# Unused pads in on-chip memory, so that the operands of the float32r products start 128 bytes apart, modulo 256

## The chip, the cores and the metric

The kernel runs on one core of a Trainium2 chip. The time is device time in microseconds (us), from the first to the last instruction of that core and the little that lies around them; lower is better. Everything on the chip that this text speaks of is inside one core: the tensor engine (PE), which multiplies matrices; the vector engine (DVE), ScalarE (ACT) and GpSimd (POOL), which work element by element; the queues that start transfers (SP and others); and the on-chip memory of 128 partitions, in which every tile has a start address that is the same in all partitions.

## The reference

Two layers of a decoder trunk on 512 tokens of 1024 channels, in float32. Cut to what matters here:

```python
for i in range(DEPTH):                                  # 2 layers
    n = rmsnorm(h, mix_norm[i])
    u = n @ w_in[i]                                     # 1024 -> 2304, four token mixers
    a_val, a_gate, pool_in, q, k, v, gb, gc, sv = jnp.split(u, IN_SPLITS, axis=-1)
    ...
    mixed = jnp.concatenate([y_a, y_b, y_c, y_d], axis=-1)
    h = h + mixed @ w_out[i]
    h = h + hier_moe(rmsnorm(h, ffn_norm[i]), ...)      # 16 experts of width 256, two per token
    gate = jax.nn.sigmoid(rmsnorm(h, ple_norm[i]) @ ple_gate_w[i] + ple_gate_b[i])
    h = h + gate * (p[i] @ ple_proj[i])
return rmsnorm(h, final_norm)
```

## The kernel before

Large products are made in float32r: each operand is split in two tiles, hi (the rounded value) and lo (the rest), and one product becomes three matmuls (`mm3`, lines 247 to 250): hi by hi (line 248), hi by lo (249) and lo by hi (250). Each matmul first loads a stationary operand of 128 columns and then streams the moving operand, 512 columns (or 256 in the first projections and for v), past it into a bank of results.

Weights come from DRAM in units of [128, 2048], through rings of buffers `wr` (`wraw`, and up to three more rings while the experts run). ScalarE makes `wh` from a half of a unit (`whi_of`, line 221) and DVE makes `wl` as the difference (`wlo_of`, line 232). There are four `wh` and four `wl` tiles of 4096 bytes per partition, in the pools `whi` and `wlo`, and the stream `_Weights.get` makes them a few halves ahead.

A layer has these stages, and the products in them are:

- `project`: the normed input `nhi`, `nlo` by the weights. The channel-major part (`cm_half`) has the weights stationary and `nhi`/`nlo` moving; v, q and k have it the other way round. Between the products DVE does the convolution's taps (line 474).
- `attend`: attention, and the output projection between its steps, with `mhi`/`mlo` stationary and the weights moving.
- `experts`: for each of 16 experts eight chunks of gate and up weights by the gathered rows `xTh`/`xTl` (24 matmuls, rows stationary), then the down product, of which the first chunk is split (`hh` stationary, 6 matmuls) and the second is plain float32 (line 1231).
- `combine`: the embedding's gate, with `n3h`/`n3l` stationary and the weights moving.

The order on every engine is written out by hand in tables and doesn't depend on addresses. Addresses come from tile pools, which are stacked from either end of the memory. `base`, `gpool`, `small`, `wraw`, `whi` and `wlo` lie on the left and stay open throughout; the pools of the stages lie behind them on the left, or on the right. `self.side` says which, and it is turned round after each layer (line 355: `self.side = self.side[::-1]`), so what lies left in layer 0 lies right in layer 1.

Of the kernel before, what the change touches and what calls it, by code (L numbers as in the profile page):

```python
# [11 lines left out]
F32 = mybir.dt.float32  # L12
# [21 lines left out]
# columns of the packed per-layer parameters  # L34
# [4 lines left out]
# columns of the shape constants  # L39
K_ID, K_RC, K_IO, K_VT, K_DE, K_IW, K_MK, K_TRI, K_COS, K_SIN = 0, 128, 160, 288, 304, 320, 322, 450, 578, 834  # L40
NCON, NCON2, NCON3 = 322, 256, 512
NOIDX = 2048.0
BUDGET = 3.1
# [7 lines left out]
# the order in which work is issued: of an attention step, of the last steps, of the layer's end  # L51
# [18 lines left out]
class _Pool:  # L70
    """A tile pool that is opened at once and closed by name."""
# [12 lines left out]
class _Weights:  # L84
    """The stream of weight units, in the order in which they are used.

    A unit is [128, 2048] in DRAM. A split half is handed out as a pair of float32r tiles (hi, lo)
    whose sum is the weight; what is left of the unit is handed out as it is.
    """
# [10 lines left out]
    def add(self, src, split=2, gain=None):  # L100
        """split: of the halves, how many; gain: called for a column of factors for each quarter of the unit."""
        u = len(self.units)
        self.units.append((src, split))
        self.gains[u] = gain
        self.items += [(u, a) for a in range(split)] + [(u, None)] * (split < 2)
# [41 lines left out]
class _Ticks:  # L147
    """Work for later ticks, and background work that is dealt out by its length."""
# [18 lines left out]
class _Kernel:  # L167
# [7 lines left out]

    def mm(self, shape, dt=F32):
        return self.ps.tile(shape, dt, name="mm", tag="mm", bufs=8 - self.ntr - self.attn)
# [4 lines left out]
    def banks(self, ntr, attn=0):  # L182
        """The PSUM's banks anew: ntr for transposes, one for attention's result, the others for products."""
        if self.ps:
            self.ps.close_()
        self.ntr, self.attn = ntr, attn
        self.ps = self.pool("ps", space=PSUM)

    # ---- small pieces
# [10 lines left out]
    def rms(self, i):  # L200
        """1 / rms of the rows of token tile i."""
        ss = self.sm.tile([128, 1], F32, name="ss", bufs=4)
        self.SC.activation(self.junk, self.h[i], AF.Square, accum_out=ss)
        r = self.sm.tile([128, 1], F32, name="r", bufs=4)
        self.rsq(r, ss, 1.0 / D)
        return r
# [45 lines left out]
    # ---- the whole  # L252
    def run(self):
# [5 lines left out]
        self.rings = []  # L259
        self.whi = self.pool("whi", 4)  # L260
        self.wlo = self.pool("wlo", 4)
        self.ps = None
# [9 lines left out]
        # the functions' table is loaded, and the tensor engine's clock up, by the time the data is there  # L272
# [68 lines left out]
        for p in (self.dram, self.ps, self.wlo, self.whi, ring, self.sm, self.gpool, base):  # L341
            p.close_()
# [18 lines left out]
    def params(self, l):  # L361
        V, SC, P = self.V, self.SC, self.P
        lam_init = 0.8 - 0.6 * math.exp(-0.3 * l)
        sm = self.sm
        self.cwh = sm.tile([128, 2, 31], F32, name="cwh", bufs=1)
        V.tensor_scalar(self.cwh, P[:, C_CW:C_CW + 62].rearrange("p (m k) -> p m k", m=2), 0.5, None, op0=ALU.mult)
        lgh = sm.tile([128, 4], F32, name="lgh", bufs=1)
        V.tensor_scalar(lgh, P[:, C_LG:C_LG + 4], 0.5, None, op0=ALU.mult)
        self.lg, self.lb = lgh[:, 0:2], lgh[:, 2:4]
        self.sgl = sm.tile([128, 1], F32, name="sgl", bufs=1)  # L370
        V.tensor_scalar(self.sgl, P[:, C_SG:C_SG + 1], 1.0 - lam_init, None, op0=ALU.mult)
        lamp = self.xp.tile([128, 2, 32], F32, name="lamp", bufs=1)
        lv = P[:, C_LAM:C_LAM + 128].rearrange("p (c a d) -> p c a d", c=2, a=2)
        V.tensor_mul(lamp, lv[:, :, 0], lv[:, :, 1])
        lam2 = sm.tile([128, 2], F32, name="lam2", bufs=1)
        V.tensor_reduce(lam2, lamp, axis=AX, op=ALU.add)
        SC.activation(lam2, lam2, AF.Exp)
        self.nlam = sm.tile([128, 1], F32, name="nlam", bufs=1)
        V.tensor_sub(self.nlam, lam2[:, 1:2], lam2[:, 0:1])
        V.tensor_scalar(self.nlam, self.nlam, -lam_init, None, op0=ALU.add)  # L380
        self.pbs = sm.tile([128, 2], F32, name="pbs", bufs=1)
        V.tensor_mul(self.pbs, P[:, C_PB:C_PB + 2], P[:, C_PS:C_PS + 2])
        self.cb = P[:, C_CB:C_CB + 2]
        self.psc = P[:, C_PS:C_PS + 2]
        self.sw = P[:, C_SW:C_SW + 6].rearrange("p (m k) -> p m k", m=2)
        self.rb = P[:, C_RB:C_RB + 20]
        self.pw = P[:, C_PW:C_PW + 256].rearrange("p (m c) -> p m c", m=2)
        # the router's weights, times the gain of the norm before it
        self.rw = P[:, C_RW:C_RW + 160].rearrange("p (c e) -> p c e", c=8)
        V.tensor_mul(self.rw, self.rw, P[:, C_FN:C_FN + 8, None].to_broadcast([128, 8, 20]))  # L390

    # ---- input projection; the channel-major mixers
# [9 lines left out]
    def cm_first(self, o, halves, toks):  # L402
        """As cm_half for both halves, the products of the high parts before the others."""
# [18 lines left out]
    def project(self):  # L422
# [3 lines left out]
        # conformer gate and value, the first two token tiles before the others  # L426
# [59 lines left out]
        # pooling mixer  # L486
# [4 lines left out]
        sums = []  # L491
# [47 lines left out]
        # short gated convolution  # L539
# [35 lines left out]
        # v, q and k by token; rotary  # L575
# [41 lines left out]
        def rotate(i, b):  # L617
            """Rotary on a token tile's q or k; the first tile is read where the products stand."""
# [18 lines left out]
    def layer_norm(self):  # L637
        """LayerNorm over the channels of the convolution's result, and silu, tile by tile in stages."""
        V, T, SC, tk, acc, sm = self.V, self.T, self.SC, self.ticks, self.acc, self.sm
        mv, rs, th = {}, {}, {}  # L640
        # token-major values stand in the tile's own columns once these are transposed
# [41 lines left out]
    # ---- differential attention, with the output projection between  # L683
    def attend(self):
# [9 lines left out]
        # a head's 32 channels of q, split, stand as hi, lo, hi, and those of k as hi, hi, lo  # L694
# [85 lines left out]
        def comb(n):  # L780
            """The difference of the two softmaxes, times the first one's sum."""
# [72 lines left out]
        def fn2(i):  # L854
            """The rows of the normed tile, for the experts' gathers."""
            p, tag = ((self.gpool, "gv0"), (xp, "qks"), (tp, "xn"), (xp, "xt"))[i]
            xx = self.scaled(i, rr[i], gffn, p, 1, "xn", tag)
            SC.dma_start(xnd[i * 128:(i + 1) * 128, :], xx)

        def fn3(i, b=None):  # L860
            """The tile itself transposed, for the router, whose result is scaled afterwards."""
# [18 lines left out]
        # the pieces of the output projection, each in two halves, and the step from which each may go  # L880
# [5 lines left out]
        def filler(n, k):  # L886
            """Up to k half pieces."""
# [38 lines left out]
        def turns(n):  # L926
            if n == NS:
                kp.close_()
                self.mp = self.pool("mp", side=self.side[0])
                self.open_ring(NRING2, 0, NRING2)  # L930
# [32 lines left out]
        # the last tile, whose chain of results the rest gives way to  # L963
# [49 lines left out]
    def open_ring(self, n, side, first):  # L1013
        """More room for weights, up to the end of the experts."""
        w, end = self.w, self.moe_end[self.l]
        if not self.rings:
# [3 lines left out]
            def pick(u):  # L1020
                """The room that is free first, of that which is there; the last units leave the first ring."""
# [10 lines left out]
    def warm(self, k):  # L1032
        """Products that only keep the tensor engine's clock up where it would wait."""
# [4 lines left out]
    # ---- routing  # L1038
# [3 lines left out]
    def first_max(self, dst, src, n, nm):  # L1042
        """One-hot of the first largest of each n groups' four elements, and the largest."""
# [10 lines left out]
    def route(self):  # L1054
# [10 lines left out]
        # the first largest of the groups, and the first two of every group's experts  # L1065
# [12 lines left out]
        # pc: of the tokens before, how many go to each expert; last, of all tokens  # L1078
# [5 lines left out]
        # what a slot shall know of its token: the rows in xnd and in yd, less NOIDX  # L1084
# [20 lines left out]
        # blocks past the first 128 rows of an expert  # L1105
# [15 lines left out]
    def weights(self):  # L1121
        """Weights of a token's two experts."""
# [20 lines left out]
    def block(self):  # L1143
        """The next block past the first rows: its tokens' rows in xnd and yd, and its expert."""
# [15 lines left out]
        # block cnt holds the pairs with ob = cnt + 1 that are past their expert's first rows  # L1160
# [35 lines left out]
    def silu(self, gu):  # L1196
        """2 silu(gate) * up."""
# [7 lines left out]
    def down_in(self, hs, split=True):  # L1205
        """The hidden values transposed, the first half of the channels in two parts."""
# [12 lines left out]
    def down(self, hT, w_, first=None):  # L1219
        """Half of the product with the down weights, w_(chunk) each; or the first chunk's two parts."""  # L1220
# [49 lines left out]
    # ---- the experts, on the first 128 rows of each  # L1270
# [47 lines left out]
    # ---- combine, per-layer embedding gate, and the next norm  # L1318
    def combine(self):
# [10 lines left out]
        def proj(k):  # L1330
            """The embedding's projection, halved, in pieces."""
# [42 lines left out]
        def norm2(i):  # L1374
            """1 / rms of the rows again, from the sums of the halves."""
# [191 lines left out]
```

## Time and profile before

| | |
|---|---|
| Time, median of 3 runs (lowest to highest) | 928.54 us (927.61 to 929.37) |
| Span of the profiled execution | 928.2 us |
| PE busy | 860.4 us (93%) |
| DVE busy | 715.7 us (77%) |
| ScalarE busy | 520.2 us (56%) |
| GpSimd busy | 150.0 us (16%) |
| Moved by DMA | 179.02 MB, 193 GB/s over the span |
| TensorE clock granted, mean | 0.971 of full speed |

How to read it: the profile is one execution, taken by the hardware profiler. Matmuls are pipelined, so that the next one starts long before the one before it has ended; the busy time of a group is the sum of durations shared out where they overlap, and "mean ns" is the duration of one. PEld is the load of the stationary operand, which runs beside matmuls. PEclk is the granted clock of TensorE, 1.00 or 0.50 of full speed (2.4 or 1.2 GHz). The span is divided between the two layers at about 467 us: layer 0's projection from 15 to 126 us, attention to 237, experts to 390, the rest to 467, and then the same again.

### The profile page before, as it was taken

What the parts mean: (1) busy time and instruction counts of PE and PEld (TensorE: products, weight loads), DVE (VectorE), ACT (ScalarE), POOL (GpSimd) and SP (SyncE); (2) the same over time, 40 slices, a digit from 0 to 9 for tenths busy, and PEclk for the clock granted to TensorE, in tenths of its full rate; (3) what the DMA queues carried; (4) which work ended last, traced back from release to release, by engine and by line L of the source; (5) the groups of instructions that cost most, each with busy time, mean ns of one, the idle gap of its engine ahead of it and who ended that gap; (6) DMA issues with size and microseconds to landing.
All of it is one profiled execution on the core that took longest, in us unless ns stands there. A gap on an engine that the chain in (4) does not pass through costs nothing. (4 is left out here: it accounts for less than half of the span.)

```text
span 928.2 us, 12348 instructions
## 1 busy us (share of the span) xinstructions
PE 860.4 (93%) x4393; PEld 687.8 (74%) x4393; DVE 715.7 (77%) x1182; ACT 520.2 (56%) x945; POOL 150.0 (16%) x214
## 2 busy tenths in 40 slices
PE   7999988897899999989979999989969999998994
PEld 5888876686677777767879887767847777776783
DVE  4599989966788888746676998998478888885674
ACT  4322246863687878745433232488337778786453
POOL 1040001122322211101010400022131222111201
PEclk8999999998999999999999999999979999999998
DMA  9322330148799979663322223110968998873602
GB/s 351 107 91 91 102 113 1 46 175 324 265 336 373 360 281 336 227 231 146 114 91 91 91 90 108 64 46 25 350 232 304 368 374 318 324 304 99 249 24 90
DMA packets 35775, 179.02 MB, mean 193 GB/s; under 512 B 8064, under 2 KB 8320, under 8 KB 18944
## 3 DMA queue, kind: packets, MB, share of 16 engines
q1 hardware_dynamic: 23472, 148.49, 42.8%
q0 software_dynamic: 9792, 20.99, 6.1%
q10 hardware_dynamic: 2448, 8.73, 2.6%
q8 instruction: 35, 0.57, 0.2%
q14 instruction: 28, 0.23, 0.1%
HBM read 171.89 MB, written 23.07 MB: 210 GB/s over the span
## 5 line engine op out<-in xcount | busy, mean ns | idle before, releaser
L232 DVE TENSOR_TENSOR wl<-wr,wh 128x1024 fp32r<-128x1024 f32 x212 | 253.3, 1221 | 42.8 <-ACT wh L221 41.7
L221 ACT CAST wh<-wr 128x1024 fp32r<-128x1024 f32 x212 | 216.4, 1053 | 93.1 <-PE mm L249 61.8
L248 PE MATMUL mm<-wh,xTh 128*128 128x512 f32 x256 | 114.8, 448 | 1.0 <-ACT xTh L214 1.0
L474 DVE SCALAR_TENSOR_TENSOR acc<-glu,cwh,acc 128x512 f32<-128x512 f32 x120 | 100.5, 837 | 3.4
L250 PE MATMUL mm<-wh,xTl 128*128 128x512 f32 x256 | 101.3, 396 | 1.1 <-DVE xTl L215 1.1
L249 PE MATMUL mm<-wl,xTh 128*128 128x512 f32 x256 | 99.7, 390 | 0.0
L250 PE MATMUL mm<-nhi,wl 128*128 128x512 f32 (+1 forms) x224 | 78.1, 349 | 2.6 <-DVE wl L232 2.6
L248 PE MATMUL mm<-nhi,wh 128*128 128x512 f32 (+1 forms) x224 | 78.0, 348 | 0.0
L249 PE MATMUL mm<-nlo,wh 128*128 128x512 f32 (+1 forms) x224 | 77.7, 347 | 0.0
L248 PEld LDWEIGHTS mm<-wh,xTh 128*128 128x128 f32 x256 | 48.2, 188 | 16.2 <-issue 6.7
L1231 PE MATMUL mm<-wr,hT 128*128 128x512 f32 x128 | 60.1, 591 | 0.0
L249 PEld LDWEIGHTS mm<-wl,xTh 128*128 128x128 f32 x256 | 48.3, 189 | 15.1 <-DVE wl L232 6.2
L1188 POOL DMA_INDIRECT xg<-xnd,ix x32 | 35.1, 1097 | 149.6 <-PE tr L244 136.8
L250 PEld LDWEIGHTS mm<-wh,xTl 128*128 128x128 f32 x256 | 48.0, 188 | 13.7 <-DVE xTl L215 2.9
L248 PE MATMUL mm<-wh,mhi 128*128 128x512 f32 x128 | 54.0, 422 | 1.0 <-DVE h L741 1.0
L1193 POOL DMA_INDIRECT yd<-ys,ix x32 | 32.3, 1011 | 122.5 <-ACT ys L1233 106.9
L248 PE MATMUL mm<-wh,n3h 128*128 128x512 f32 x128 | 51.4, 402 | 0.0
L249 PE MATMUL mm<-wl,n3h 128*128 128x512 f32 x128 | 50.7, 396 | 0.0
L250 PE MATMUL mm<-wh,n3l 128*128 128x512 f32 x128 | 50.7, 396 | 0.0
L250 PE MATMUL mm<-wh,mlo 128*128 128x512 f32 x128 | 50.4, 393 | 0.0
L249 PE MATMUL mm<-wl,mhi 128*128 128x512 f32 x128 | 50.0, 391 | 0.0
L250 PEld LDWEIGHTS mm<-nhi,wl 128*128 128x128 f32 x224 | 42.8, 191 | 8.6 <-DVE wl L232 3.2
(236 smaller groups left out, 1859.5 us busy)
## 6 DMA issues: line engine op xcount, KB each, us to landing
wr<-wgu SPq DMA_DIRECT2D x62, 1024.0 KB, 8.1
wr<-wdn SPq DMA_DIRECT2D x30, 1024.0 KB, 13.0
wr<-win SPq DMA_DIRECT2D x13, 1024.0 KB, 5.7
wr<-wout SPq DMA_DIRECT2D x8, 1024.0 KB
wr<-wpg SPq DMA_DIRECT2D x8, 1024.0 KB, 12.0
yt<-yd SPq DMA_DIRECT2D x12, 512.0 KB
wr<-wqk SPq DMA_DIRECT2D x4, 1024.0 KB, 4.8
xnd<-xn ACTq DMA_DIRECT2D x8, 512.0 KB, 8.3
```

Of the source, the lines that this page charges most:

```text
L221: self.SC.copy(hi, src)
L232: self.V.tensor_sub(lo, src, h32)
L248: self.T.matmul(o, lh, rh, start=first, stop=False)
L249: self.T.matmul(o, lh, rl, start=False, stop=False)
L250: self.T.matmul(o, ll, rh, start=False, stop=last)
L474: V.scalar_tensor_tensor(acc[:, m], glu[:, m, k:k + S], self.cwh[:, m, k:k + 1], acc[:, m], op0=ALU.mult, op1=ALU.add)
L1188: return self.G.indirect_dma_start(out=dst, out_offset=None, in_=self.xnd[:, :], in_offset=bass.IndirectOffsetOnAxis(ap=col, axis=0), boun ...
L1193: return self.G.indirect_dma_start(out=self.yd[:, :], out_offset=bass.IndirectOffsetOnAxis(ap=col, axis=0), in_=src, in_offset=None, bound ...
L1231: self.T.matmul(o[nh], hT[:, c], wc[:, ns], start=(c == 0), stop=(c == 1))
```

## The change

Four tiles are added that nothing writes or reads, and the pools that hold them. They move the start of everything that is allocated behind them.

```diff
+PAD_L, PAD_W, PAD_R, PAD_M = 352, 128, 224, 160
...
+    def pad(self, name, n, side):
+        p = self.pool(name, side=side)
+        p.tile([128, n // 4], F32, name=name)
+        return p
...
         ring = self.pool("wraw", NRING)
         self.rings = []
+        pads = [self.pad("padl", PAD_L, "left"), self.pad("padr", PAD_R, "right")]
         self.whi = self.pool("whi", 4)
         self.wlo = self.pool("wlo", 4)
+        padw = self.pad("padw", PAD_W, "left")
...
-        for p in (self.dram, self.ps, self.wlo, self.whi, ring, self.sm, self.gpool, base):
+        for p in (self.dram, self.ps, padw, self.wlo, self.whi, *pads, ring, self.sm, self.gpool, base):
...
                 kp.close_()
                 self.mp = self.pool("mp", side=self.side[0])
+                self.mp.tile([128, PAD_M // 4], F32, name="padm")
```

The diff also takes out comments, by which line numbers shift. The instructions of the built program, their order on each engine and the semaphores and values for which they wait are the same before and after; only addresses differ. These are the remainders of the start addresses, modulo 256:

| tiles | before, layer 0 | before, layer 1 | after, both layers |
|---|---|---|---|
| `wh`, `wl` | 32 | 32 | 128 |
| `nhi`, `nlo` (projection) | 224 | 32 | 0 |
| `mhi`, `mlo` (output projection) | 32 | 224 | 0 |
| `xTh`, `xTl`, `hh` (experts) | 32 | 224 | 0 |
| `n3h`, `n3l` (gate) | 128 | 128 | 0 |
| `KT`, `QT` (scores) | 224 | 32 | 0 |

Every chunk that a matmul reads starts a multiple of 512 bytes into its tile, so these remainders hold for all of them. While one matmul streams its moving operand, the stationary operand of the next is loaded. The distance between the two (start of the next stationary operand less start of the moving one, modulo 256) is then:

| products | before, layer 0 | before, layer 1 | after |
|---|---|---|---|
| channel-major projection | 64 | 0 | 128 |
| v, q and k | 192 | 0 | 128 |
| output projection, experts | 0 | 192 | 128 |
| gate | 96 | 96 | 128 |

All of these tiles but n3h and n3l start at an odd multiple of 32 bytes before; after, all start at a multiple of 128. The later rings of `wr` move too (from remainders 32, 128 and 224 to 0); the first one, h and the constants stay.

## Rows read from the trace of the kernel before

**Rows 1.** The page: busy time, share and instructions; GB/s in 40 slices.

```profile
PE 860.4 (93%) x4393; PEld 687.8 (74%) x4393; DVE 715.7 (77%) x1182; ACT 520.2 (56%) x945; POOL 150.0 (16%) x214
...
GB/s 351 107 91 91 102 113 1 46 175 324 265 336 373 360 281 336 227 231 146 114 91 91 91 90 108 64 46 25 350 232 304 368 374 318 324 304 99 249 24 90
```

**Rows 2.** PE's groups by shape, line 248: count, busy us, mean ns, idle before.

```profile
L248 PE MATMUL mm<-wh,xTh 128*128 128x512 f32 x256 | 114.8, 448 | 1.0 <-ACT xTh L214 1.0
...
L248 PE MATMUL mm<-wh,mhi 128*128 128x512 f32 x128 | 54.0, 422 | 1.0 <-DVE h L741 1.0
L248 PE MATMUL mm<-wh,n3h 128*128 128x512 f32 x128 | 51.4, 402 | 0.0
...
L248 PE MATMUL mm<-nhi,wh 128*128 128x512 f32 x128 | 50.2, 392 | 0.0
...
L248 PE MATMUL mm<-wh,hh 128*128 128x512 f32 x64 | 27.6, 432 | 1.3 <-ACT hh L214 1.3
...
L248 PE MATMUL mm<-wh,nhi 128*128 128x512 f32 x64 | 25.1, 392 | 0.0
```

**Rows 3.** Stretches: length, busy us (instructions) of each engine, PEclk, DMA share, GB/s.

```profile
core 0: us, PE busy (x) PEld busy (x) DVE busy (x) ACT busy (x) POOL busy (x), PEclk, DMA share, GB/s
44.00:84.00 40.00, 40.00 (x173) 32.25 (x172) 38.22 (x49) 9.32 (x11) 9.87 (x12) 1.00 0.26 94
101.00:121.00 20.00, 20.00 (x89) 16.42 (x88) 19.37 (x30) 5.05 (x9) 0.00 (x0) 1.00 0.26 97
500.00:540.00 40.00, 40.00 (x178) 33.15 (x177) 38.34 (x50) 9.33 (x11) 10.03 (x12) 1.00 0.24 86
...
431.00:457.00 26.00, 26.00 (x113) 20.90 (x111) 18.00 (x26) 11.90 (x24) 0.93 (x3) 1.00 0.27 101
885.00:911.00 26.00, 26.00 (x112) 20.91 (x111) 18.26 (x26) 14.33 (x28) 2.35 (x6) 1.00 0.06 21
...
126.00:237.00 111.00, 96.42 (x578) 77.33 (x578) 87.20 (x215) 64.04 (x165) 22.34 (x36) 0.94 0.34 129
...
254.00:381.00 127.00, 127.00 (x575) 96.28 (x573) 109.35 (x153) 99.06 (x147) 24.34 (x24) 1.00 0.89 333
...
31.00:41.00 10.00, 10.00 (x90) 10.00 (x90) 3.09 (x9) 4.19 (x6) 0.00 (x0) 1.00 0.22 91
...
544.00:554.00 10.00, 10.00 (x85) 10.00 (x85) 8.55 (x13) 4.66 (x7) 0.00 (x0) 1.00 0.25 92
...
482.70:485.30 2.60, 2.60 (x14) 2.60 (x14) 1.99 (x11) 0.20 (x1) 0.00 (x0) 0.50 0.75 236
```

**Rows 4.** Time line of PE, an expert of each layer: start us, duration us, engine, line.

```profile
274.35 0.40 PE L249 MATMUL mm<-wl,xTh 128*128 128x512 f32 x1
...
276.67 0.39 PE L250 MATMUL mm<-wh,xTl 128*128 128x512 f32 x1
...
277.35 0.39 PE L249 MATMUL mm<-wl,xTh 128*128 128x512 f32 x1
...
279.64 0.40 PE L250 MATMUL mm<-wh,xTl 128*128 128x512 f32 x1
...
728.92 0.39 PE L249 MATMUL mm<-wl,xTh 128*128 128x512 f32 x1
...
731.21 0.40 PE L250 MATMUL mm<-wh,xTl 128*128 128x512 f32 x1
```

**Rows 5.** Time line of all engines: the load beside the first matmul of rows 4.

```profile
274.36 0.19 PEld L250 LDWEIGHTS mm<-wh,xTl 128*128 128x128 f32 x1
```

**Rows 6.** Time line of PE at the half clock: first and last of twelve in a row.

```profile
483.02 0.41 PE L250 MATMUL mm<-nhi,wl 128*128 128x256 f32 x1
...
485.37 0.41 PE L249 MATMUL mm<-nlo,wh 128*128 128x256 f32 x1
```

**Rows 7.** DVE's groups by shape, 254 to 381 and 709 to 836 us.

```profile
L232 DVE TENSOR_TENSOR wl<-wr,wh 128x1024 fp32r<-128x1024 f32 x66 | 78.5, 1222 | 8.5 <-ACT wh L221 8.5
...
L232 DVE TENSOR_TENSOR wl<-wr,wh 128x1024 fp32r<-128x1024 f32 x67 | 79.5, 1220 | 8.2 <-ACT wh L221 8.2
```

## The prediction

> **What bounds the kernel now.** Four views, in this order. The page's busy times: TensorE (PE) is busy 860.4 of 928.2 us, VectorE (DVE) 715.7 [rows 1]. The groups of PE by shape: the split products of lines 248 to 250 are 2304 matmuls that are 512 columns wide. Of each group of line 248 that is shown, 249 and 250 have as many: 768 with xTh or xTl, 384 with mhi or mlo, 384 with n3, 384 of the channel-major projection, 192 of q and k; 192 with hh come on top [rows 2]. Another 288 a layer, by the code, are 256 wide. A group's mean (392 to 448 ns) is the duration of one, and they overlap, so it isn't what one costs. The stretches: in the projection, the experts and the gate PE is busy 100% of the time and waits for nothing [rows 3]. There a product costs its spacing, the time from one start to the next, and that is the quantity which this change can move: instructions, their order and all waits are the same before and after, and only addresses differ.
>
> **Spacing by place.** In a full stretch, spacing = (length + 0.39) / count, because a product that began up to 0.39 us earlier is counted too; one count more or less is 1.3 ns in 40 us and 2.5 in 20. The same code at the same clock (PEclk 1.00) gives [rows 3]: input projection, layer 0 (distance 64): 40.39/173 = 233.5 ns; layer 1 (distance 0): 40.39/178 = 226.9; q and k of layer 0 (distance 192): 20.39/89 = 229.1; gate (distance 96 in both layers): 26.39/113 = 233.5 and 26.39/112 = 235.6, together 234.5. In the experts ten spacings take 2.32 and then 2.29 us in layer 0 (distance 0, a new chain after every pause) and 2.29 in layer 1 (distance 192) [rows 4]: 230.5 and 229.0. Between the layers the two sides of the memory swap; the code is one. So spacing depends on where the operands lie.
>
> **Why it may.** The load of the next stationary operand starts 0.01 us after the matmul before it (274.36 after 274.35) [rows 4, 5], so two reads run side by side: 2048 bytes per partition of the moving operand and 512 of the stationary one. At the half clock, where columns come at 1.2 per ns, eleven spacings of 256-wide products take 2.35 us, 213.6 each, which is 256/1.2 = 213.3 and nothing more [rows 3, 6]. At 2.4 columns per ns, 512 should take 213.3 too, and float32r loses 13.6 ns at distance 0, 20.2 at 64, 21.2 at 96, 15.8 at 192. At distance 0 that is 32 or 33 columns, some 128 bytes, and at 64 it is 48 columns, 192 bytes: what it takes for the moving read to fall back until it lies half of 256 bytes from the other one. Read so, the two streams meet in one half of a 256-byte period, one waits until they are in opposite halves, and a start at 128 would need no waiting. I choose this reading. No row shows distance 128, so I keep both ends.
>
> By the Trainium skill, page "SBUF — State Buffer", section "Who interferes with whom", TensorE has separate read ports for the moving operand and for the weight load, and it never waits on anyone; by that rule distance does nothing and the sum is zero. The two layers' 233.5 and 226.9 ns [rows 3] speak against it, yet it is a rival below.
>
> **The change part by part.** Pads add no instruction and no DMA. *Bounds of the new spacing:* below, 213.3 + 0.3 as at the half clock, 213.6; above, 234.5, the spacing at the nearest distance. I take 218, nearer to the lower end (an estimate: that end, and a few ns for chains that start anew after each pause, which in layer 0's experts cost 2.32 against 2.29 us [rows 4]). *Projection, 512 wide:* layer 0: 192 x 15.5 = 3.0 us and 96 x 11.1 = 1.1; layer 1: 288 x 8.9 = 2.6. PE is released there by DVE's wl tiles, and DVE is nearly full: 38.22 and 38.34 of 40 us, 19.37 of 20 [rows 3]. Over 44.8, 65.3 and 22 us that leaves it 2.0, 2.7 and 0.7, so of 6.7 us I keep 2.0 + 0.7 + 2.5 = 5.2. *Experts:* 16 x (24 + 6) = 480 products a layer: 480 x 12.5 = 6.0 and 480 x 11.0 = 5.3. DVE is busy 109.35 of 127 us, so it doesn't stop this; DMA is next, at a share of 0.89 and 333 GB/s [rows 3], which would have to become 0.93 and some 350. Slices of the page reach 374 GB/s [rows 1]. I keep nine tenths: 10.2. *Gate:* 384 x 16.5 = 6.3, with DVE at 18 of 26 us [rows 3]: all of it. *Output projection:* 384 products at distances 0 and 192, taken like the experts': 384 x 11.8 = 4.5; they fill in between the steps of attention, where PE is busy 96.42 of 111 us [rows 3], so the chain of softmax takes back part; half: 2.2. *256 wide:* weight loads are busy 10.00 of 10.00 us there, so the load sets the pace: 10.28/90 = 114 ns at distance 64, 10.28/85 = 121 at 0 [rows 3]. At best 7 ns in some 400 of them, 2.8 us; at worst nothing; I take 1.0. *DVE and ScalarE* read and write the same tiles at new places, but the split of a weight takes DVE 1222 and 1220 ns in the two layers' experts, whose buffers lie differently [rows 7]: nothing. KT and QT move by the same amount.
>
> Sum: 5.2 + 10.2 + 6.3 + 2.2 + 1.0 = 24.9 us. The profiled execution's span is 928.2, the median of the runs 928.54; taken from the median, 903.6.
>
> **Rivals.** *No place is better than the best one seen.* The 13.6 ns at distance 0 are what float32r costs at this clock wherever it lies, and only what stands above goes: 226.9 everywhere. Layer 0's projection gives 192 x 6.6 + 96 x 2.2 = 1.5, the experts 480 x 3.6 + 480 x 2.1 = 2.7, the gate 384 x 7.6 = 2.9, the output projection half of 384 x 2.9 = 0.6, the narrow ones 1.0: 8.7 us, so 919.8. For it: distance 0 is the lowest of four, and stands close to 192's 229. Against it: at half the clock such a cost doesn't show [rows 6].
>
> *128 is near the worst place.* The nearest row to 128 is 96, and it is the slowest seen; going by rows alone, spacing climbs from 0 to 96 and at 192 has come down most of the way. A straight line from 96 to 192 gives 234.5 - 5.4/3 = 232.7 at 128. Then layer 1's projection loses 288 x 5.8 = 1.7 us, the experts 480 x 2.2 + 480 x 3.7 = 2.8, the output projection half of 384 x 2.9 = 0.6, layer 0's q and k 0.3, while layer 0's projection and the gate get back 0.2 + 0.7: 4.5 us, 933.0. If 128 costs what 96 does, 2.2 + 4.6 + 0.9 + 0.5 + 0.2 = 8.4 us, 936.9. It decides from a spacing of about 230.5, today's mean (576 in the projections at 226.9 to 233.5, 1344 at about 230, 384 at 234.5). That a loss which rises towards 128 should vanish there is my reading's weak point: by it 96 should cost 56 columns, 23.3 ns, and shows 21.2, and 192 should cost less than 0 does and costs more.
>
> *It does nothing.* Spacing goes with something else in which the layers differ, the side rather than the remainder, and the new remainders leave it alone: 928.5. The skill's page would give the same time.
>
> **How the numbers follow.** Chances: no collisions at 128, 0.45 (903.6); a floor of 226.9, 0.18 (919.8); near the worst, 0.25 (933.0 to 936.9); nothing, 0.12 (928.5). The first two are faster by over 0.2% (1.9 us, about what a measurement of this kernel can tell from no change): 0.63; same 0.12; slower 0.25. The range: with 216 in place of 218 the first case gains 2304 x 2 = 4.6 us more, and some 4 of what I took off come back if DVE and DMA keep up, so 895; at the other end it goes to 935, between the two prices of the slow case. Outside stay a larger gain (0.07) and half of the slow case (0.12).
>
> **What would show it.** In the profile after, the spacing in the middle of the projection, the experts and the gate, which should be one in both layers, since the distance is. 214 to 219 confirms the reading, 226.9 the floor, 232 and more the slow case; layers that still differ would show that the remainder of 256 wasn't the cause. Where spacing falls but the time doesn't, PE would show new waits for wl in the projection, or for what DMA brings in the experts. If the split's duration on DVE moved, I would have left out an engine.

## The result, and the profile after

Times are medians over many executions. The changed kernel takes 932.79 us (median of 20 runs, 929.78 to 937.46), the kernel before 927.53 in the same comparison (20 runs, 925.57 to 933.57): 1.0054 times as long, with a 95% interval of 1.0042 to 1.0066. It is slower by some 5 us. The forecast was 903.6; the rival "128 is near the worst place" had 933.0.

The page of the changed kernel: the span, and the busy time of each engine. Instructions and DVE's work are what they were in [rows 1]; PE has a little more to do.

```profile
span 929.9 us, 12348 instructions
...
PE 863.1 (93%) x4393; PEld 686.9 (74%) x4393; DVE 716.3 (77%) x1182; ACT 518.9 (56%) x945; POOL 149.8 (16%) x214
...
L239 DVE TENSOR_TENSOR wl<-wr,wh 128x1024 fp32r<-128x1024 f32 x212 | 253.4, 1221 | 42.3 <-ACT wh L228 41.3
```

The stretches of the changed kernel that answer to [rows 3], with the same columns (length; busy us and count of each engine; PEclk; DMA share; GB/s). The gate is read at 433 and 887 us here, since it begins 2 us later.

```profile
31.00:41.00 10.00, 10.00 (x86) 10.00 (x86) 2.92 (x8) 4.00 (x5) 0.00 (x0) 1.00 0.18 73
44.00:84.00 40.00, 40.00 (x174) 32.43 (x173) 38.24 (x49) 9.30 (x11) 9.90 (x12) 1.00 0.25 93
101.00:121.00 20.00, 20.00 (x88) 16.22 (x87) 19.36 (x30) 5.28 (x9) 0.00 (x0) 1.00 0.26 97
254.00:381.00 127.00, 127.00 (x573) 96.18 (x573) 108.94 (x152) 98.31 (x146) 25.30 (x25) 1.00 0.89 331
433.00:459.00 26.00, 26.00 (x113) 21.07 (x113) 18.29 (x26) 12.18 (x24) 0.94 (x3) 1.00 0.28 101
500.00:540.00 40.00, 40.00 (x174) 32.44 (x173) 38.25 (x49) 9.29 (x11) 9.89 (x12) 1.00 0.25 91
709.00:836.00 127.00, 127.00 (x573) 96.21 (x572) 108.95 (x153) 98.26 (x146) 24.35 (x24) 1.00 0.89 333
887.00:913.00 26.00, 26.00 (x113) 20.90 (x112) 18.38 (x26) 14.51 (x29) 2.36 (x6) 1.00 0.05 22
```

The experts of layer 1 before, which [rows 3] do not have:

```profile
709.00:836.00 127.00, 127.00 (x577) 96.70 (x576) 109.68 (x154) 99.40 (x147) 24.44 (x24) 1.00 0.88 334
```

What to see: the two layers, which differed before (173 against 178 products in 40 us, 575 against 577 in 127 us), now agree, 174 and 174, 573 and 573, 113 and 113. The spacing is 40.39/174 = 232.1 ns in both projections, 20.39/88 = 231.7 for q and k, 26.39/113 = 233.5 in the gates. In layer 1's experts ten spacings take 2.32 us, where [rows 4] had 2.29 (time line of PE: start, duration, line):

```profile
730.28 0.39 PE L256 MATMUL mm<-wl,xTh 128*128 128x512 f32 x1
...
732.60 0.40 PE L257 MATMUL mm<-wh,xTl 128*128 128x512 f32 x1
```

Where the 5 us come from, stage by stage, as products times the change of spacing:

| stage | products | before, ns | after, ns | us |
|---|---|---|---|---|
| layer 0, channel-major, 512 wide | 192 | 233.5 | 232.1 | -0.3 |
| layer 0, channel-major, 256 wide (an estimate: those that follow each other without waits) | 120 | 10.28/90 = 114.2 | 10.28/86 = 119.5 | +0.6 |
| layer 0, q and k | 96 | 229.1 | 231.7 | +0.2 |
| layer 1, channel-major, q and k | 288 | 226.9 | 232.1 | +1.5 |
| experts, both layers (some 150 us each: 150 x 2/575 + 150 x 4/577, from the counts in 127 us) | | | | +1.6 |
| gate | 384 | 234.5 | 233.5 | -0.4 |
| output projection, half of it on the path (an estimate: rates of the experts) | 384 | 229.8 | 232.0 | +0.4 |

That is 3.6 of the 5.0 us (3.9 to 6.1 by the interval); a count that is off by one shifts a row of the table by 0.3 to 0.8. Added up start by start over both traces, the experts' split products lost 2.0 us and not 1.6 (120.2 and 119.7 us before, 121.0 in each layer after). The rest is not accounted for.

The two profiled spans differ by 1.7 us only. One reason is that the execution of before had a piece at the half clock at the start of layer 1's projection that the one of after did not have (the same stretch of before and then of after, PEclk 0.57 and 1.00). The eleven spacings of [rows 6] alone, at 213.6 ns instead of some 120, are 1.0 us (an estimate).

```profile
482.00:486.00 4.00, 3.65 (x18) 3.66 (x19) 2.69 (x12) 0.46 (x2) 0.00 (x0) 0.57 0.66 225
```

```profile
482.00:486.00 4.00, 3.08 (x23) 2.70 (x24) 3.82 (x10) 2.27 (x4) 0.00 (x0) 1.00 0.19 33
```

### The profile page after: what moved, and what is told of

Same layout as the page of the kernel before. It is cut to its first block, busy times and chain, and to the rows that moved or that the text cites. A ratio compares the mean times of both kernels' runs of the same rounds, so it can differ in the third digit from the quotient of the medians.

```text
span 929.9 us, 12348 instructions
## 1 busy us (share of the span) xinstructions
PE 863.1 (93%) x4393; PEld 686.9 (74%) x4393; DVE 716.3 (77%) x1182; ACT 518.9 (56%) x945; POOL 149.8 (16%) x214
## 5 line engine op out<-in xcount | busy, mean ns | idle before, releaser
L239 DVE TENSOR_TENSOR wl<-wr,wh 128x1024 fp32r<-128x1024 f32 x212 | 253.4, 1221 | 42.3 <-ACT wh L228 41.3
```

The lines of the kernel that those rows point to most:

```text
L239: self.V.tensor_sub(lo, src, h32)
```

## Every distance, alone on the chip

Theory after the result: spacing goes by the distance of the operands modulo 256, and 128 is simply a bad one. The first rival: it goes by the place or by the alignment. The second: nothing collides, and some part of the loss belongs to any float32r product. The first experiment leaves out the computation and measures the disputed cost by itself: chains of 60 matmuls, each with one pair of start addresses, and nothing beside them.

```diff
+RUNS = [(f"d{d}x", 0, d, 512, 128, F32R) for d in (0, 16, 32, 48, 64, 80, 96, 112, 128, 144, 160, 176, 192, 208, 224, 240, 256)]
...
+        for j in range(N):
+            m = m0 // e + (j % 4) * 512
+            s = half + s0 // e + (j % 8) * 128
+            nc.tensor.matmul(acc[:c, :w], t[:, s:s + c], t[:, m:m + w], start=(j == 0), stop=(j == N - 1))
```

> This kernel leaves out the whole computation: it runs chains of 60 matmuls with nothing else beside them, each chain with one pair of start addresses, and copies x to the output. DISTANCE (the spacing of 512-wide float32r products depends on the distance of the two operands modulo 256 and on nothing else of the address): 226.7 ns at distance 0, 233.3 at 64, 234.3 at 96, 232.4 at 128, 228.9 at 192, as measured in the kernel; between them about 230 at 32, 230.5 at 160, 228 at 224; 256 gives what 0 gives; with both operands moved by 32, 64 or 128 the same values; 256-wide 120.0 at 0 and 113.3 to 118 at 64. If the loss is a collision of the stationary load with the moving read, a stationary operand of 64 columns should halve it (220 at distance 0, 224 at 96) and one of 32 columns quarter it (217 and 218). PLACE (the side or the surroundings set it): chains at one and the same place of memory show one spacing at all distances, near 230. FLOOR (13 ns are what float32r costs whatever is loaded): 226.7 at distance 0 with 64 and 32 columns too.

Time line of PE, one row for each chain: start, duration of the whole chain, name, shapes, count. d is the distance; m64 and m128d128 have the moving operand at 64 and 128 (distances 0 and 128); c64 and c32 load 64 and 32 stationary columns; n has 256 moving columns; b is bf16. Spacing = (duration of the chain less that of its last product) / 59; the last product takes 0.39 us, 0.28 in n and 0.38 in b.

```profile
54.38 13.77 PE L48 MATMUL d16x<-q 128*128 128x512 f32 x60
67.99 14.15 PE L48 MATMUL d32x<-q 128*128 128x512 f32 x60
...
123.89 14.22 PE L48 MATMUL d96x<-q 128*128 128x512 f32 x60
...
151.95 14.16 PE L48 MATMUL d128x<-q 128*128 128x512 f32 x60
...
207.74 13.90 PE L48 MATMUL d192x<-q 128*128 128x512 f32 x60
...
235.47 14.16 PE L48 MATMUL d224x<-q 128*128 128x512 f32 x60
...
263.09 13.76 PE L48 MATMUL d256x<-q 128*128 128x512 f32 x60
276.69 13.80 PE L48 MATMUL m64x<-q 128*128 128x512 f32 x60
...
317.93 14.16 PE L48 MATMUL m128d128x<-q 128*128 128x512 f32 x60
...
339.13 7.23 PE L48 MATMUL n64x<-q 128*128 128x256 f32 x60
346.20 7.29 PE L48 MATMUL n128x<-q 128*128 128x256 f32 x60
...
360.39 13.96 PE L48 MATMUL c64d0x<-q 128*64 128x512 f32 x60
374.19 13.76 PE L48 MATMUL c64d96x<-q 128*64 128x512 f32 x60
...
428.49 13.11 PE L48 MATMUL b64x<-b 128*128 128x512 bf16 x60
...
467.15 14.19 PE L48 MATMUL d8x<-q 128*128 128x512 f32 x60
```

Of the multiples of 16, distances 256 (that is 0), 16 and 240 give 226.6 to 227 ns (the chain d0, the first of float32r, has 230.7, since its first spacing is 418 ns and the next ones vary from 224 to 236 before they settle at 226.7), 192 gives 229.0, 176 gives 230.0, and all the others 232.0 to 234.4: 128 is 233.4, 96 is 234.4, 32 and 224 are 233.2 and 233.4. But 0 is no valley between 240 and 16: at 8 and 248 the spacing is 233.9 and 233.4, and the second sweep's distances of 4 to 28, none a multiple of 16, gave 230.0 to 235.1. The four distances that the kernel before happened to show were two of the good ones and two of the bad ones. Moving both operands changes 1 ns at most (227.3 in m64, 233.4 in m128d128). The chains lie at one place of memory and still differ, so it isn't the place. At the distances that the kernels show, the 512-wide values are those of the kernel within some 1 ns, so DVE, ScalarE and the DMA queues, which are at work there, make no difference that shows. bf16 takes 215.8 to 216.1 at all four distances that were run.

The 256-wide products do not fit so well. Alone they take 117.8 ns at distance 64 and 118.8 at 128, a loss of 1.0 where the table above has 5.3. The kernel before itself shows two values at distance 64: 114.2 from 31 to 41 us, and 2.71/23 = 117.8 a little earlier:

```profile
22.31 0.28 PE L248 MATMUL mm<-nhi,wh 128*128 128x256 f32 x1
...
25.02 0.28 PE L250 MATMUL mm<-nhi,wl 128*128 128x256 f32 x1
```

So their 0.6 us was measured in the kernel, but that the distance made it is not shown.

Three expectations fell. Lines drawn between the kernel's four distances (230 at 32, 228 at 224) are wrong. And fewer stationary columns do not take the loss away: with 64 of them distance 0 gets worse (230.0) and distance 96 better (226.6). A collision whose size is the bytes of the load cannot do that, and a floor of 226.7 at distance 0 whatever is loaded (FLOOR) doesn't hold either: with 32 columns it has 231.7.

## Widths, columns and restarts

> As the first sweep, this leaves out the whole computation: chains of float32r matmuls. r chains stop after 24 matmuls until VectorE has rewritten their first stationary operand, three times at each distance; w and v chains have moving operands of 128 to 512 columns at distance 0 and 96, c and e chains stationary operands of 1, 16, 96 and 128 columns at distance 0 and 96, f chains distances 4 to 28. COLLISION BY BYTES (what is lost is proportional to what is read): the loss at 128 columns of moving operand is a quarter of that at 512, 3.4 ns at distance 0, and with one stationary column it is gone (213.6 ns for 512 columns). FIXED LOSS PER MATMUL (16 to 48 columns of time for each matmul, in steps of 16, whatever it reads; the first sweep showed 32 columns for 256 and for 512 columns at distance 0, and no less with 64 or 32 stationary columns): distance 0 gives (w + 32) / 2.4, that is 66.7 ns at 128 if the load of 188 ns does not set the pace, 173 at 384, 200 at 448 and 226.7 at 512, and one stationary column still 226 to 233. RESTARTS: at distance 0 the first ten spacings after a pause average 230 as in the experts, then 226.7; if another distance (16 and 240 reached 226.7 in the first sweep) shows no such start, it would be the better one for the experts.

```diff
+RUNS += [(f"w{w}x", 0, 0, w, 128, 48, 0) for w in (128, 192, 256, 320, 384, 448, 512)]
+RUNS += [(f"v{w}x", 0, 96, w, 128, 48, 0) for w in (128, 192, 256, 320, 384, 448, 512)]
+RUNS += [(f"c{c}x", 0, 0, 512, c, 48, 0) for c in (1, 16, 96, 128)]
```

The same view; here spacing = (duration - 0.39) / 47. w chains are at distance 0, v chains at 96. The last product is shorter in narrower chains: 0.31 us at 320 columns, 0.33 at 384, some 0.37 at 448. The r chains begin anew after a pause, with a first spacing of 0.34 us: (duration - 0.39 - 0.34) / 22.

```profile
46.77 5.73 PE L48 MATMUL r0x<-q 128*128 128x512 f32 x24 [0.32 <-DVE q L43]
...
58.88 5.71 PE L48 MATMUL r16x<-q 128*128 128x512 f32 x24 [0.32 <-DVE q L43]
64.90 5.86 PE L48 MATMUL r16x<-q 128*128 128x512 f32 x24 [0.32 <-DVE q L43]
...
351.89 7.21 PE L48 MATMUL w320x<-q 128*128 128x320 f32 x48
...
367.26 10.08 PE L48 MATMUL w448x<-q 128*128 128x448 f32 x48
...
404.52 7.21 PE L48 MATMUL v320x<-q 128*128 128x320 f32 x48
...
419.89 9.76 PE L48 MATMUL v448x<-q 128*128 128x448 f32 x48
...
440.73 11.28 PE L48 MATMUL c1x<-q 128*1 128x512 f32 x48
```

The loss is one for each matmul, not one for each byte. Above the columns by 2.4 per ns it is 13.4 ns at 320 and at 384 columns as it is 13.3 at 512 ((7.21 - 0.31) / 47 = 146.8, and (8.48 - 0.33) / 47 = 173.4), and with a single stationary column 512 columns still take 231.7. From 128 to 256 columns the spacing is 110 to 120 ns, nearly whatever the width, so something else than the columns sets the pace there. In columns the loss is mostly near 32 (13.3 ns) or 48 (20 ns).

Which of the two comes up is not the distance's alone. At 320 columns distances 0 and 96 take the same (146.8), and at 448 distance 0 has 206.6, where FIXED LOSS had 200, and distance 96 has 200.0, the other way round from 512. Restarts decide too. At distance 0 both restarts gave 227.3 ((5.73 - 0.73) / 22). At 16, which had looked as good, one gave 226.4 and two 233.2; at 144 it was 226.4 once and 233.6 twice; 240 stayed between 227.7 and 229.1. So of the three good distances only 0 kept its value.

## Where the loss sits

> Chains of 48 float32r matmuls again, the computation left out, at distances 0, 96 and 128. plain: as in the first sweep. same: the moving operand is always the same 512 columns. again: it is 128 columns read four times. one: one column read 512 times. two: every other column of 1024. k64, k32: 64 and 32 partitions. swap: two result banks in turn. MEMORY (what is lost is lost where the moving operand is read): one column read 512 times loses no more than bf16 does (216 ns) at all distances, again lies between, and two (4096 bytes passed over) costs more than plain. TENSOR ENGINE (a fixed loss for each float32r matmul, whatever is read): 226.7, 234.3 and 232.4 to 233.4 at distances 0, 96 and 128 in all of them. Number of partitions and of result banks should change nothing by either.

```diff
+            if kind == "one":
+                mov = q[:k, m:m + 1].to_broadcast([k, 512])
+            if kind == "two":
+                mov = q[:k, m:m + 1024].rearrange("p (n t) -> p n t", t=2)[:, :, 0]
```

```profile
102.04 11.06 PE L53 MATMUL again0x<-q 128*128 128x512 f32 x48
112.93 11.40 PE L53 MATMUL again96x<-q 128*128 128x512 f32 x48
...
135.33 10.65 PE L53 MATMUL one0x<-q 128*128 128x512 f32 x48
145.82 10.66 PE L53 MATMUL one96x<-q 128*128 128x512 f32 x48
156.32 10.66 PE L53 MATMUL one128x<-q 128*128 128x512 f32 x48
166.81 21.82 PE L53 MATMUL two0x<-q 128*128 128x512 f32 x48
...
283.52 20.68 PE L53 MATMUL k32d96x<-q 32*128 32x512 f32 x48
```

When the moving operand is one column read 512 times, a product takes (10.65 - 0.38) / 47 = 218.5 ns, and distance makes no difference any more (10.65, 10.66, 10.66 us). So most of the loss (all but 2.7 ns above bf16), and all of its dependence on these three distances, needs a moving operand that is read on from column to column. Every other column of 1024 takes twice as long, (21.82 - 0.63) / 47 = 450.9. 128 columns read four times (again) cost what 512 different ones do, 227.0 and 234.3, and at distance 96 the chains with 64 partitions and with two result banks took the same 11.40 us. Neither reading came as expected: again was to lie between one and plain by MEMORY, and by TENSOR ENGINE one and two were to cost what plain does. The k32 chains at distances 96 and 128 ran at the half clock, and there 512 columns at distance 96 take (20.68 - 0.62) / 47 = 426.8 ns, which is 512/1.2 and no loss at all, as [rows 6] showed for 256. It isn't the 32 partitions: swap0, with 128, began at the half clock, and its spacings there, after the first, are 426 to 427 ns as well. The stretch of the k32 chain at distance 96:

```profile
285.00:303.00 18.00, 18.00 (x43) 13.77 (x43) 0.00 (x0) 0.00 (x0) 0.50 0.00 1
```

## Back in the kernel: distance 128 in another place, 32, and 0

> PAD_L 384 and PAD_R 192: everything moves by 32 bytes, so operands start at odd multiples of 32 again as in the kernel before, and the distance is 128 as in the changed kernel. DISTANCE: 232.4 ns in all stages and 932.8 us, as in the changed kernel. ALIGNMENT (what slowed the changed kernel is that all operands start at multiples of 128 bytes): spacings fall back to what the kernel before shows or below, 218 to 230, and the time to 928 us or less.

```diff
-PAD_L, PAD_W, PAD_R, PAD_M = 352, 128, 224, 160
+PAD_L, PAD_W, PAD_R, PAD_M = 384, 128, 192, 160
```

933.02 us, 1.0055 of before (1.0036 to 1.0073): the changed kernel's time, at starts that are odd multiples of 32 again. Its projections, with the columns of the stretches above:

```profile
44.00:84.00 40.00, 40.00 (x174) 32.43 (x173) 38.24 (x49) 9.29 (x11) 9.89 (x12) 1.00 0.23 82
...
500.00:540.00 40.00, 40.00 (x173) 32.18 (x172) 38.22 (x50) 9.30 (x11) 9.87 (x12) 1.00 0.23 79
```

Alignment is not what slowed the kernel. Then one part of the change was undone, the pads around the weights' buffers:

> PAD_L 256 and PAD_W 224: one part of the change undone, the weights' buffers lie at remainder 32 as in the kernel before, all else at 0 as in the changed kernel. Distance 32 in the channel-major projection, 224 in all other products. CURVE (the spacings of the first sweep hold in the kernel, 233.4 at 32 and 233.3 at 224): about 1 ns above the changed kernel in all stages, 1440 x 1.0 = 1.4 us, some 934 us, 1.006 to 1.007 of before. STRAIGHT LINES between the four distances of the kernel before (230 at 32 and 228 at 224): faster than the changed kernel by 3 to 4 us, 929 us or less.

```diff
-PAD_L, PAD_W, PAD_R, PAD_M = 352, 128, 224, 160
+PAD_L, PAD_W, PAD_R, PAD_M = 256, 224, 224, 160
```

933.19 us, 1.0058 (1.0039 to 1.0077); 40.39/173 = 233.5 ns and 40.39/174 = 232.1 in the projections, 26.39/113 = 233.5 in the gate. The values measured alone hold in the kernel, and the straight lines do not.

```profile
44.00:84.00 40.00, 40.00 (x173) 32.22 (x172) 38.22 (x50) 9.31 (x11) 9.88 (x12) 1.00 0.23 80
...
500.00:540.00 40.00, 40.00 (x174) 32.23 (x173) 38.24 (x47) 10.27 (x12) 9.76 (x11) 1.00 0.28 103
434.00:460.00 26.00, 26.00 (x113) 20.89 (x112) 18.33 (x26) 12.41 (x25) 1.03 (x4) 1.00 0.27 101
```

Distance 0 everywhere was run twice, the second time beside a version with 192 in the experts:

> PAD_L 224 and PAD_W 256: only the weights' buffers move, and all operands start at 0, so distance 0 in all stages. DISTANCE: spacing 226.7 ns in the projection and the gate of both layers, 229 to 230.6 over the short chains of the experts; against the changed kernel 576 x 5.7 = 3.3 us in the projections, 960 x 2.4 = 2.3 in the experts, 384 x 5.7 = 2.2 in the gate, half of 384 x 4 = 0.8 in the output projection, 0.3 lost where products are 256 wide: 8.3 us, 924.5 us, 0.996 to 0.997 of the kernel before. PLACE (the spread of spacings is not the distance's): 232.4 ns stays in all stages, 932.8 us.

> The second experiment once more, on the same chip as the mixed distances, to tell a difference of 0.1% from none: 926.6 us and 0.9986 of before if it holds, with an interval that leaves 1 out.

```diff
-PAD_L, PAD_W, PAD_R, PAD_M = 352, 128, 224, 160
+PAD_L, PAD_W, PAD_R, PAD_M = 224, 256, 224, 160
```

926.6 us, 0.9986 of before (0.9972 to 0.9999), and 925.81 us, 0.9974 (0.9959 to 0.9989). Stretches of the first of the two: projection of both layers, the gate of layer 0.

```profile
44.00:84.00 40.00, 40.00 (x178) 33.13 (x177) 38.33 (x49) 9.79 (x12) 10.04 (x12) 1.00 0.28 98
...
498.00:538.00 40.00, 40.00 (x179) 33.10 (x178) 38.34 (x50) 9.32 (x11) 10.04 (x12) 1.00 0.22 79
...
430.00:456.00 26.00, 26.00 (x117) 21.48 (x116) 18.20 (x26) 12.54 (x25) 1.16 (x4) 1.00 0.29 101
```

226.9 and 225.6 ns in the projections and 225.6 in the gate, as expected within a count (one count is 1.3 ns in 40 us and 2 in 26); DVE is busy 38.33 of 40 us and still keeps up. This version is faster than both kernels, by some 0.2% than the one before and 0.7% than the changed one: 6 to 7 us, of an expected 8.3. The experts gave less than was expected, 573 to 575 or 576 products in 127 us, and the 256-wide products of layer 0 take 10.28/85 = 120.9 ns, where the changed kernel has 119.5 and the one before 114.2. The chains alone have the same 120.0 ns for narrow products at distance 0; they do not show what made 114.2 in the kernel before. Experts of both layers and 256-wide products, of the second run:

```profile
254.00:381.00 127.00, 127.00 (x575) 96.40 (x574) 109.33 (x154) 98.95 (x147) 24.34 (x24) 1.00 0.88 334
709.00:836.00 127.00, 127.00 (x576) 96.57 (x575) 108.77 (x152) 98.96 (x146) 24.92 (x25) 1.00 0.89 333
31.00:41.00 10.00, 10.00 (x85) 10.00 (x85) 2.56 (x4) 4.14 (x5) 0.00 (x0) 1.00 0.12 49
```

> Distance 0 as in the second experiment, but 192 in the experts (an unused tile of 192 or 64 bytes in their pool). The experts' split products took 149.4 us at 192 in layer 1 of the kernel before, and 149.8 in both layers at distance 0, as chains start anew after each pause: 0.4 us less in each layer, 0.8 below the second experiment, some 925.5 us, 0.997 to 0.998 of before. If a restart costs the same at both distances, 960 x 2.2 = 2.1 us more than at distance 0, 928.5.

```diff
+        if self.side[1] == "left":
+            ep.tile([128, 48], F32, name="pade", bufs=1)
...
+        if self.side[1] == "right":
+            self.ep.tile([128, 16], F32, name="pade", bufs=1)
```

926.39 us, 0.9978 (0.9962 to 0.9993), with 576 products in both experts' stretches: no different from distance 0. Chains that start anew lose at distance 0 what 192 loses in the steady state, so the 0.8 us did not show: in the trace of distance 0 the second to eighth spacing after a pause are 227 to 236 ns and only the later ones 226 to 227, and an expert's chains with xTh and xTl are mostly twelve products long.

## Why the prediction was wrong

**What bounds the kernel, and that spacing is the quantity: right.** The change moved addresses only, it made the spacings of the layers alike, and the time followed the spacings [rows 3]. That addresses set it, and not the side, is shown by both layers and by chains at one place. With this the rival *it does nothing* falls too: the interval of 1.0042 to 1.0066 leaves 1 out.

**The step that failed is the lower bound, and the reading it was chosen for.** "A start at 128 would need no waiting" was an extrapolation: the losses at 0 and 64 were read as bytes by which one stream falls back until the two are in opposite halves of 256. From this came 213.6 as the lower end and 218 as the value. Measured: 232.1 to 233.5 in the kernel, 232.5 to 233.4 alone. The reading needs a loss that grows with the overlap of two reads; one stationary column (231.7 ns) and the moving widths (13.3 to 13.4 ns at 320, 384 and 512) show a loss for each product instead, which 128 does not take away. What sets its size stays open. The prediction had named the two points against its reading, 96 and 192, and set them aside; the row nearest to 128, 96 with 234.5, was off by 1 to 2 ns.

**The rival "128 is near the worst place" was right in sign and size:** 933.0 by the straight line, with 232.7 ns, against 932.79 and 232.1 to 233.5. Its reason, a smooth climb from 0 to 96 and a descent to 192, was not: between the kernel's four distances the multiples of 16 lie on a plateau of 232 to 234.4, except 16, 240, 176 and 192, and the line hit 128 by luck, as 32 and 224 show. Of its terms, layer 1's projection came as worked out (1.5 for 1.7), the experts lost some 1.6 to 2.0 (2.8), the gate gave back 0.4 (0.7), and the loss of the 256-wide products, 0.6, was not in it.

**The floor was a good rival for the wrong layout.** 226.9 is the best that any distance gave, so "no place is better than the best one seen" holds as far as was measured; but this change does not reach it. Distance 0 does in the projection and the gate, and brought 1.3 to 2.4 us against before (0.9986 and 0.9974) where 8.7 were forecast for it. Its 8.7 had 2.7 for the experts, at 226.9 ns, and they gave nothing (575 and 576 products against 575 and 577): layer 0's had distance 0 already, and their short chains never come down to 226.9 on the mean. The narrow products, forecast to gain 1.0, cost 120 x 6.7 = 0.8.

**The 256-wide products** had been bounded by 0 from below in cost. They lost 0.6 us, as 114.2 ns went to 119.5. The two values of the prediction, 114 at distance 64 and 121 at 0, already allowed for a loss, and the bound should have reached to it. Why the kernel before ran at 114.2 there is open, since the chain alone takes 117.8 at that distance.

**DVE** was costed at nothing, and the split takes 1221 ns as before [rows 7]. **DVE as the next limit** never came into play: at 226.9 ns it kept up in both layers.

The Trainium skill, page "SBUF — State Buffer", section "Who interferes with whom", says that TensorE never waits on anyone; by the prediction's reading of it, distance would do nothing. Of other engines the runs show nothing against it. But by its own operands' addresses TensorE takes 226.7 to 234.4 ns for the same product, and with one column re-read 218.5 at all three distances. The page "TensorE: Matmul & The Clock Gate", section "Wait — 56ns, not 53.3ns?", has a fixed cost of some 6 array cycles for each matmul that shows at the full clock alone. The bf16 chains agree: 215.8 ns are 518 cycles for 512 columns. For float32r the runs here show the same kind of cost, fixed and gone at the half clock, but mostly 32 to 51 cycles of it.

What stays open: whether two reads meet at all, and why the loss is near 32 or 48 columns. The runs tell that most of it needs the moving operand's read and that it goes neither by the bytes of the load nor by the width.

## What to carry to other kernels

Two measured points of a curve and a mechanism that fits them are not a third point: take the nearest row as the value, and let the mechanism move the chance. Where a change only moves addresses, measure the disputed cost alone first; one short run of bare chains here gave all distances at once. For float32r products of 512 moving and 128 stationary columns that follow one another without waits, start both operands at the same remainder modulo 256, and expect about 3% between the best and the worst place. For other shapes measure first: with 448 moving columns, or with 64 stationary ones, distance 96 was better than 0.

## What the runs showed that was not expected

- A float32r product of 512 columns costs 226.7 ns at distance 0 in the steady state and 234.4 at the worst multiple of 16 at the full clock, bf16 215.8 to 216.1 at every distance that was run; at the half clock float32r loses nothing (426.8).
- The loss is one for each product, 13 to 21 ns; it does not go away with fewer stationary columns, from 128 down to 1.
- A moving operand with every other column costs 450.9 ns, twice the plain one; one with a single repeated column 218.5.
- Some distances have two steady states: at 16 the same chain ran at 226.4 or at 233.2 ns, at 144 at 226.4 or 233.6, from one restart to the next.
